# Latents' first norm written into the context's tiles, pinned squares and weight additions, and a last column block in two halves, in one transformer layer

## The chip, the cores and the metric

The kernel runs on one core of one Trainium2 chip. The metric is the device time of one execution in microseconds (us); the time before is 2582.37 us, the median of three runs from 2581.23 to 2585.36. The profile was taken from one further execution of 2582.33 us.

## The reference, cut to what matters

One layer of a hybrid backbone works on two streams of 256 tokens, the latents `x` and the context `ctx`, with 2048 features each:

```python
D_MODEL = 2048; SEQ = 256; CTX_LEN = 256; D_FF = 5632
def adaln(x, g, mod, i):
    return rms_norm(x, g) * (1 + mod[:, i + 1, None, :]) + mod[:, i, None, :]
def half_step_ffn(x, mod, i, g, w_up, w_down):
    h = adaln(x, g, mod, i)
    a, b = jnp.split(h @ w_up, 2, axis=-1)
    return x + 0.5 * mod[:, i + 2, None, :] * ((jax.nn.silu(a) * b) @ w_down)
...
xl = half_step_ffn(xl, mod_l, 0, g_norm[l, 0], w_ffn1_up[l], w_ffn1_down[l])   # FFN1, latents
xc = half_step_ffn(xc, mod_c, 0, g_norm[l, 0], w_ffn1_up[l], w_ffn1_down[l])   # FFN1, context
hl = adaln(xl, g_norm[l, 1], mod_l, 3)       # the second norm: input of the mixer
hc = adaln(xc, g_norm[l, 1], mod_c, 3)
...
xl = half_step_ffn(xl, mod_l, 6, g_norm[l, 2], w_ffn2_up[l], w_ffn2_down[l])   # FFN2, latents only
return rms_norm(xl, g_final)
```

`mod` is a vector of nine rows of 2048 per stream, each row a product of a condition vector with a weight matrix `w_mod`. Everything is float32.

## The kernel before, in words

**Precision and splits.** Each float32 operand of a matmul is split into a high and a low part, and each product is made of three matmuls (`mm3`: high by high, low by high, high by low). A weight tile of 128 x 2048 is split by `split` (L122) in two halves of 128 x 1024: ScalarE (ACT) copies the high part `hi` (L130), VectorE (DVE) subtracts it from the source into the low part `lo` (L131). TensorE (PE) takes the two parts as stationary operands: it can't run a low-part matmul before the `lo` of that half is done. Both `hi` and `lo` have four buffers.

**FFN1** (about 150 to 1060 us of the span) multiplies the up-projection as a seven-product scheme over 2x2 blocks. `quad(n)` runs over seven sums of activations (`a11`, `a12`, `n1`, `s4`, `s2`, `s3`, `a22`), each with two tiles of weights (`q` = 0, 1), which are also sums of weight blocks. Most of the weight sums are made by a DMA that adds into the tile in SBUF (`accum`, L742, on GpSimd's queue), some by DVE in halves of 1024 columns (`summed`, L912, its addition is recorded at L848). While this goes on, DVE also multiplies the modulation rows of `w_mod` (`sraw<-in_w_mt`, loads at L239 on SP's queue; two DVE operations of 128 x 1024 per load at L210, writing `junk`). Those run beside the matmuls, one item per step of the quad.

**FFN1's down-projection** ends in `last_pair` (about 1250 to 1370 us). `acc` holds four row tiles of 128 x 2048: tiles 0 and 1 are the context, 2 and 3 the latents. When a column block of a latents' tile is final, `kept` stores it to DRAM (`x1d<-acc`), since the latents' residual is read again later, and `stat` adds up its squares on ScalarE (`sumsq`, L163, recorded at L165, writing `junk`). `latents(c)` does both for the latents' tiles 2 and 3.

**The second norm** is `adaln(s)` (L1133), with s = 0 for the context and s = 1 for the latents: a reduction of the sums of squares on DVE (L1136, L1137), a power on GpSimd (POOL, L1138), then the tiles multiplied by the reciprocal root, the left half of each row tile on DVE (L1145), the right half on ACT (L1143), in place. `to_hT` transposes the result on PE in groups of eight 128 x 128 blocks (L378), and `affine_split` applies scale and shift, half of a group on ACT (L389) and half on DVE (L390), and splits the outcome (ACT L392 `hhi`, DVE L393 `hlo`). Matmuls of the mixer's input projection run between the groups. The context is normalised first; its tiles of `acc` are not read after its transposes.

**FFN2** (about 1930 to 2550 us) has its own `quad(n)`, nine of them; the sums of weights are made by `first`, `chained` and `accum` (DMA) and by `summed_half` (L2267, on DVE, recorded at L2212). The two pairs of weight tiles (`chain20/chain21` and `ra0/ra1`) change their places from one quad to the next, so that the profile writes `chain<-chain,ra` in one quad and `ra<-ra,chain` in the next. Between the quad's steps lie the matmuls of the down-projection of earlier blocks (`mm<-hi,hid2h`, with weights split from `raw`).

**The tail** is `last2`: for the last hidden blocks, the down-projection of two row tiles (t) in four column blocks of 512 (cb). For each block there are 12 matmuls, then DVE multiplies by the gate (`half_gated`, L1045, writing `sab`), adds into `acc2` (L2458), ACT adds up the squares (L165), and DVE multiplies the block before by the final gain (`gain`, L2426). When all four blocks of a row tile are done, `ended` reduces the four sums (L2431), adds the epsilon (L2433), has POOL take the power (L2434), scales the four blocks by the outcome (L2439, L2441 on DVE, L2443 on ACT) and stores them (L2444).

**What sets the order.** A scheduler orders the instructions of each engine by its own estimate of readiness, except those that `pin` or `pinned` (`keep_in_program_order`) hold in the order in which the code issues them. An addition or a square that isn't pinned may thus be put between the two halves of a split, or ahead of it.

Of the kernel before, what the change touches and what calls it, by code (L numbers as in the profile page):

```python
# [9 lines left out]
F32 = mybir.dt.float32  # L10
# [3 lines left out]
AF = mybir.ActivationFunctionType  # L14
# [46 lines left out]
def tile_layer(ctx: ExitStack, tc: tile.TileContext, I: dict, out: bass.AP):  # L61
# [13 lines left out]
    def bank():  # L75
        return ps["mm"].tile([P, 512], F32, tag="mm", name="mm")
# [85 lines left out]

    def sumsq(dst, x, n=512):  # L163
        junk = sm.tile([P, 512], BF16, tag="junk", name="junk", bufs=1)
        scalar[0].activation(junk[:, :n], x, AF.Square, accum_out=dst)  # L165

    def normalised(x, ss4, act=False):

# [170 lines left out]
    def pin(ins):  # L339
        tc.keep_in_program_order(ins)  # L340
# [30 lines left out]
    def to_hT(xs, n, s, hhi, hlo, c0, ks=range(KT)):  # L371

        for k0 in ks[::2]:
            tb = tbank()
            for kk in range(2):
                for t in range(2):
                    k = k0 + kk
                    tensor[0].transpose(tb[:, kk * 256 + t * P : kk * 256 + (t + 1) * P], xs[t][:, k * P : (k + 1) * P], ident)  # L378
            affine_split(tb.rearrange("p (k c) -> p k c", k=2), n, ((k0, s), (k0 + 1, s)), hhi[:, k0 : k0 + 2, c0 : c0 + 256], hlo[:, k0 : k0 + 2, c0 : c0 + 256])
            yield  # L380
# [334 lines left out]
    def pinned(ins):  # L715
        tc.keep_in_program_order(ins)
# [26 lines left out]
    with pool(name="f1u", bufs=1) as f1u:  # L743
# [110 lines left out]
        def quad(n, after=lambda step: None):  # L854
# [56 lines left out]

            def summed(q, h):  # L912
                w = slice(h * 1024, (h + 1) * 1024)
                add(chain_[q][:, w], chain_[q][:, w], ra[q][:, w])

            def second(q):
                if q not in own:
                    chained(1, 2)(q)
                if q - 1 in own:
                    summed(q - 1, 0)  # L920

            def third(q):
                if q in own:
# [209 lines left out]
    def adaln(s):  # L1133

        r = sm.tile([P, 16], F32, tag="rstd", name="rstd", bufs=4)[:, :2]
        nc.vector.tensor_reduce(r, ss1[s].rearrange("p (t c) -> p t c", t=2), axis=AX.X, op=ALU.add)  # L1136
        nc.vector.tensor_scalar(r, r, 1.0 / D, EPS, op0=ALU.mult, op1=ALU.add)  # L1137
        nc.gpsimd.tensor_tensor(r, r, mhalf[:, :2], op=ALU.pow)  # L1138
        for h in range(2):
            for t in range(2):  # L1140
                x = acc[:, 2 * s + t, h * 1024 : (h + 1) * 1024]
                if h:
                    nc.scalar.activation(x, x, AF.Copy, scale=r[:, t : t + 1])  # L1143
                else:
                    nc.vector.tensor_scalar(x, x, r[:, t : t + 1], None, op0=ALU.mult)  # L1145
        yield
        yield from to_hT([acc[:, 2 * s, :], acc[:, 2 * s + 1, :]], 1, s, *hT, 256 * s)

    hT = []

    def last_pair():
# [56 lines left out]
        def stat(t, cb):  # L1208
            s, tt = divmod(t, 2)
            if s not in ss1:  # L1210
                ss1[s] = sm.tile([P, 16], F32, tag="rstd", name="ss8", bufs=4)[:, :8]
            i8 = 4 * tt + cb
            sumsq(ss1[s][:, i8 : i8 + 1], col(t, cb))

        def kept(t, cb):
            if t > 1:
# [71 lines left out]
        def latents(c):  # L1288
            for t in (2, 3):
                kept(t, 2 * c + 1)  # L1290
                stat(t, 2 * c + 1)

        def last_small():
            small.update(zip(("s3", "a22"), pair_of(slot("nl"))))
# [768 lines left out]
    with f2x:  # L2063
# [146 lines left out]
        def quad(n):  # L2210
# [55 lines left out]

            def summed_half(q, h):  # L2267
                w = slice(h * 1024, (h + 1) * 1024)
                add(chain_[q][:, w], chain_[q][:, w], ra[q][:, w])

            def early(m, q):
                if (m, q) == (3, 0):
# [137 lines left out]
        def last2():  # L2410

            parts = []
            for cb in range(NCB):
                if cb >= 2:
                    parts.append(load_split(I["w_dn2"][LAST, cb]))
                    continue
                raw = raw_tile()
                nc.sync.dma_start(raw, I["w_dn2"][LAST, cb])
                hi = f3.tile([P, 2048], F32R, tag=f"f{2 * cb}", name=f"hi{cb}")
                lo = f3.tile([P, 2048], F32R, tag=f"f{2 * cb + 1}", name=f"lo{cb}")  # L2420
                nc.scalar.activation(hi, raw, AF.Copy)
                nc.vector.tensor_tensor(lo, raw, hi.bitcast(F32), op=ALU.subtract)
                parts.append(lambda w, hi=hi, lo=lo: (hi[:, w], lo[:, w]))
            def gain(t, cb):
                a = acc2[:, t, cb * CB : (cb + 1) * CB]
                pin(nc.vector.tensor_tensor(a, a, late["gf"][:, cb * CB : (cb + 1) * CB], op=ALU.mult))  # L2426

            def ended(t, ss):

                s1 = sm.tile([P, 1], F32, tag="s1", name="s1")  # L2430
                pin(nc.vector.tensor_reduce(s1, ss, axis=AX.X, op=ALU.add))  # L2431
# [17 lines left out]
            sss = [sm.tile([P, 4], F32, tag="ss4", name="ss4", bufs=4) for _ in range(2)]  # L2449
            first = ended(0, sss[0])  # L2450
            for t in range(2):
                for cb in range(NCB):
                    c = slice(cb * CB, (cb + 1) * CB)
                    b = block(bank(), LAST, parts[cb], t)
                    a = acc2[:, t, c]
                    y = sab_tile()
                    half_gated(y, b, late["g8"][:, c])
                    nc.vector.tensor_tensor(a, a, y, op=ALU.add)  # L2458
                    sumsq(sss[t][:, cb : cb + 1], a)
                    if cb or t:  # L2460
                        gain(*divmod(4 * t + cb - 1, 4))
                    if t:
                        steps(first)
            drain(ended(1, sss[1]))
# [101 lines left out]
```

## Time and profile before

| what | value |
|---|---|
| median of three runs | 2582.37 us (2581.23 to 2585.36) |
| the profiled execution | 2582.33 us |
| its span, first to last instruction | 2580.6 us, so 1.73 us lie outside |
| granted TensorE clock, mean | 0.999 |
| DVE busy | 86% of the span |
| ACT, POOL busy | 55%, 8% |
| mean DMA rate | 259 GB/s |

In a row of the timeline the first number is the start in us from the span's start, the second the busy time, then come engine, line, operation, output and inputs by the program's names (buffer numbers left out) and shapes; a bracket at the end is idle time of the engine just before, and what ended it. `x2` merges two instructions of one kind. PE's matmuls overlap: a 128 x 512 one is listed with 0.39 us and follows the one before by about 0.227 us.

### The profile page before, as it was taken

The numbers are of one execution on the slowest core, as the hardware profiler recorded it, in microseconds if no ns is written. First come the engines' busy times: TensorE is split into PE (matmuls) and PEld (weight loads), VectorE is DVE, ScalarE is ACT, GpSimd is POOL, SyncE is SP. The second block draws the span as 40 slices with busy tenths as digits, with TensorE's granted clock in tenths as the row PEclk, the third lists the DMA queues.
The fourth block names the chain that finished last, engine by engine and source line by source line (L and its number), as shares of the span: only waits on it lengthen the run. The fifth ranks groups of instructions, "written<-read, shape, count | busy, mean of one in ns | idle before, by whom it ended". The sixth has DMA issues, their size and how long they took to land.

```text
span 2580.6 us, 33786 instructions
## 1 busy us (share of the span) xinstructions
PE 2551.6 (99%) x12462; PEld 2117.9 (82%) x12462; DVE 2215.2 (86%) x2921; ACT 1407.3 (55%) x1805; POOL 214.9 (8%) x264
## 2 busy tenths in 40 slices
PE   8999999999999999999999999999999999999998
PEld 5788888888887888888889889888898888888886
DVE  7789888888889888888896889798889888888987
ACT  5454444444444455444464347566476666666763
POOL 0000000000000000011110000120000000000001
PEclk9999999999999999999999999999999999999999
DMA  9989999999999999999686887776768999999985
GB/s 397 353 213 263 260 274 253 250 275 272 261 269 255 264 258 247 244 211 235 162 200 247 314 293 258 244 261 224 265 251 236 274 276 283 286 276 272 272 252 167
DMA packets 150022, 668.97 MB, mean 259 GB/s; under 512 B 23000, under 2 KB 43992, under 8 KB 90336
## 3 DMA queue, kind: packets, MB, share of 16 engines
q1 hardware_dynamic: 121488, 484.34, 50.8%
q0 software_dynamic: 28368, 182.46, 35.9%
q8 instruction: 98, 1.61, 0.2%
q14 instruction: 68, 0.56, 0.1%
HBM read 648.86 MB, written 17.89 MB: 258 GB/s over the span
## 4 chain that ended last, share of the span: by engine, by line
PE 82%; DVE 7%; DMA 6%; issue 4%; ACT 1%; POOL 0%; ACTq 0%; POOLq 0%; DVEq 0%
PE mm L154 59%; PE Y L154 6%; PE X L154 5%; PE tr L154 3%; PE mm L89 3%; DVE lo L131 3%; PE tr L89 1%; DMA ra<-in_w_up2b 1%; DMA mraw<-in_w_m 1%; DMA chain<-in_w_dn 1%; DMA chain<-in_w_up1b 1%; DMA sr<-in_w_mt 1%; DVE junk L210 1%; ACT hi L130 1%; DMA raw<-in_w_dn 1%
## 5 line engine op out<-in xcount | busy, mean ns | idle before, releaser
L130 ACT ACTIVATE hi<-raw 128x1024 fp32r<-128x1024 f32 (+2 forms) x476 | 490.7, 1039 | 376.7 <-PE mm L154 278.8
L131 DVE TENSOR_TENSOR lo<-raw,hi 128x1024 fp32r<-128x1024 f32 (+2 forms) x464 | 553.0, 1205 | 94.9 <-ACT hi L130 77.2
L130 ACT ACTIVATE hi<-chain 128x1024 fp32r<-128x1024 f32 x352 | 369.1, 1059 | 332.9 <-PE mm L154 185.2
L131 DVE TENSOR_TENSOR lo<-chain,hi 128x1024 fp32r<-128x1024 f32 x352 | 425.0, 1220 | 101.0 <-ACT hi L130 93.3
L154 PE MATMUL mm<-hi,hhi 128*128 128x512 f32 (+3 forms) x1024 | 390.0, 381 | 0.0
L154 PE MATMUL mm<-lo,hhi 128*128 128x512 f32 (+3 forms) x1024 | 387.3, 378 | 1.2 <-DVE lo L131 0.8
L154 PE MATMUL mm<-hi,hlo 128*128 128x512 f32 (+3 forms) x1024 | 386.3, 377 | 0.0
L210 DVE SCALAR_TENSOR_TENSOR junk<-sraw,cBh 128x1024 fp8e5<-128x1024 f32 x192 | 234.6, 1222 | 24.4 <-DMA sraw<-in_w_mt 23.2
L154 PEld LDWEIGHTS mm<-lo,hhi 128*128 128x128 f32 x1024 | 192.4, 188 | 37.6 <-DVE lo L131 4.6
L154 PEld LDWEIGHTS mm<-hi,hhi 128*128 128x128 f32 x1024 | 192.5, 188 | 32.2 <-ACT hi L130 0.7
L154 PEld LDWEIGHTS mm<-hi,hlo 128*128 128x128 f32 x1024 | 192.6, 188 | 31.9
L131 DVE TENSOR_TENSOR lo<-ra,hi 128x1024 fp32r<-128x1024 f32 x104 | 126.3, 1222 | 27.5 <-ACT hi L130 23.6
L130 ACT ACTIVATE hi<-ra 128x1024 fp32r<-128x1024 f32 x104 | 110.0, 1061 | 65.7 <-PE mm L154 39.7
L154 PE MATMUL mm<-hi,sumshl 128*128 128x512 f32 x456 | 140.4, 389 | 0.0
L154 PE MATMUL mm<-lo,hid2h 128*128 128x512 f32 x352 | 137.3, 390 | 0.1
L154 PE MATMUL mm<-hi,hid2h 128*128 128x512 f32 x352 | 137.0, 389 | 0.0
L154 PE MATMUL mm<-hi,hid2l 128*128 128x512 f32 x352 | 137.0, 389 | 0.0
L154 PE MATMUL mm<-hi,sumshh 128*128 128x512 f32 x368 | 113.3, 389 | 0.0
L210 DVE SCALAR_TENSOR_TENSOR sr<-sr,cBl 128x1024 f32<-128x1024 f32 x84 | 102.1, 1224 | 12.7 <-DMA sr<-in_w_mt 11.8
L742 POOL DMA_DIRECT2D chain<-in_w_up1b x51 | 45.0, 883 | 738.2 <-DVE lo L131 591.3
L154 PE MATMUL mm<-hhi,hi 128*128 128x512 f32 (+1 forms) x288 | 101.4, 352 | 0.0
L154 PEld LDWEIGHTS mm<-hi,sumshl 128*128 128x128 f32 x456 | 85.6, 188 | 17.7
(526 smaller groups left out, 5431.3 us busy)
## 6 DMA issues: line engine op xcount, KB each, us to landing
raw<-in_w_dn SPq DMA_DIRECT2D x64, 1024.0 KB, 10.2
chain<-in_w_up1b POOLq DMA_DIRECT2D x51, 1024.0 KB, 10.9
sraw<-in_w_mt SPq DMA_DIRECT2D x96, 512.0 KB, 7.5
sr<-in_w_mt SPq DMA_DIRECT2D x81, 512.0 KB, 5.3
raw<-in_w_up1b SPq DMA_DIRECT2D x40, 1024.0 KB, 9.5
mraw<-in_w_m SPq DMA_DIRECT2D x32, 1024.0 KB, 7.5
chain<-in_w_dn POOLq DMA_DIRECT2D x28, 1024.0 KB, 9.7
chain<-in_w_up2b POOLq DMA_DIRECT2D x28, 1024.0 KB, 11.1
```

The costliest lines, as they stand in the source:

```text
L89: ins = getattr(self.engine, name)(*a, **k)
L130: scalar[0].activation(hi, src, AF.Copy)
L131: vector[0].tensor_tensor(lo, src, hi.bitcast(F32), op=ALU.subtract)
L154: tensor[0].matmul(out_ap, s, m, start=first and not n, stop=last and n == 2, skip_group_check=skip)
L210: ins = nc.vector.scalar_tensor_tensor(junk() if junk else raw, raw, 1.0, cB[s], op0=ALU.mult, op1=ALU.mult, accum_out=mT[:, i, s, kt, h : ...
L742: accum = lambda dst, src: nc.gpsimd.dma_start(dst, src, accum_op=ALU.add)
```

## The change

It has four parts.

1. `adaln` multiplies from tile `2s + t` into tile `t` of `acc`. For the latents (s = 1) the normalised values thus go into the context's tiles 0 and 1, and the transposes read from there; for the context nothing is different.
2. The squares that `latents` issues are pinned. All that the code issues ahead of them and that is pinned stays ahead.
3. In FFN1's `quad`, the addition `summed(q - 1, 0)` is pinned, behind the split that stands ahead of it in the code. In FFN2's `quad`, the first half of the second addition, `summed_half(1, 0)`, moves from step (3, 1) to step (2, 1) and is pinned there.
4. In the tail, the last column block of the second row tile (t = 1, cb = 3) is computed in two halves of 256 columns, each with its own bank, 12 matmuls, gate and addition; the first half's squares are taken by ACT, the second half's by DVE with a multiplication that accumulates. The sum of squares has five entries in place of four.

```diff
     def sumsq(dst, x, n=512):
...
-        scalar[0].activation(junk[:, :n], x, AF.Square, accum_out=dst)
+        return scalar[0].activation(junk[:, :n], x, AF.Square, accum_out=dst)
...
             def second(q):
                 if q not in own:
                     chained(1, 2)(q)
                 if q - 1 in own:
-                    summed(q - 1, 0)
+                    pinned(summed(q - 1, 0))
...
-                x = acc[:, 2 * s + t, h * 1024 : (h + 1) * 1024]
+                w = slice(h * 1024, (h + 1) * 1024)
+                x, y = acc[:, 2 * s + t, w], acc[:, t, w]
                 if h:
-                    nc.scalar.activation(x, x, AF.Copy, scale=r[:, t : t + 1])
+                    nc.scalar.activation(y, x, AF.Copy, scale=r[:, t : t + 1])
                 else:
-                    nc.vector.tensor_scalar(x, x, r[:, t : t + 1], None, op0=ALU.mult)
+                    nc.vector.tensor_scalar(y, x, r[:, t : t + 1], None, op0=ALU.mult)
         yield
-        yield from to_hT([acc[:, 2 * s, :], acc[:, 2 * s + 1, :]], 1, s, *hT, 256 * s)
+        yield from to_hT([acc[:, 0, :], acc[:, 1, :]], 1, s, *hT, 256 * s)
...
         def latents(c):
             for t in (2, 3):
                 kept(t, 2 * c + 1)
-                stat(t, 2 * c + 1)
+                pinned(stat(t, 2 * c + 1))
...
             def late_(m, q):
                 if (m, q) == (2, 1):
+                    pin(summed_half(1, 0))
                     summed_half(0, 0)
                 elif (m, q) == (3, 0):
                     accum(ra[0], part(n, 1, 0))
-                elif (m, q) == (3, 1):
-                    summed_half(1, 0)
...
+            def halves(t, cb, ss):
+
+                w = CB // 2
+                bs = [bank()[:, :w] for _ in range(2)]
+                y = sab_tile()
+                for h, b in enumerate(bs):
+                    o = cb * CB + h * w
+                    a, z = acc2[:, t, o : o + w], y[:, h * w : (h + 1) * w]
+                    tt = slice(t * P, (t + 1) * P)
+                    for j in range(FB):
+                        m = slice(j * CB + h * w, j * CB + (h + 1) * w)
+                        mm3(b, hids[LAST][0][:, j, tt], hids[LAST][1][:, j, tt], *parts[cb](m), j == 0, j == FB - 1)
+                    half_gated(z, b, late["g8"][:, o : o + w])
+                    nc.vector.tensor_tensor(a, a, z, op=ALU.add)
+                    if h:
+                        nc.vector.scalar_tensor_tensor(z, a, 1.0, a, op0=ALU.mult, op1=ALU.mult, accum_out=ss[:, cb + 1 : cb + 2])
+                    else:
+                        sumsq(ss[:, cb : cb + 1], a, w)
+                        gain(t, cb - 1)
...
             for t in range(2):
                 for cb in range(NCB):
+                    if (t, cb) == (1, NCB - 1):
+                        steps(first)
+                        halves(t, cb, sss[t])
+                        continue
```

Lines behind L1138 have numbers larger by one in the changed kernel. What moves on the engines is seen at three places.

ScalarE around the latents' squares of column block 1 (`junk,ss<-acc`), about 1330 us, where the context's norm is still being transposed (`h`, `hhi`) and weights are split (`hi`); before:

```order
L389 ACTIVATE h<-tr,SH,SC 128x256
L165 ACTIVATE junk,ss_10185<-acc 128x512 x2
L392 ACTIVATE hhi<-h 128x2x256
L389 ACTIVATE h<-tr,SH,SC 128x256
L1280 ACTIVATE hi<-raw 128x1024
L392 ACTIVATE hhi<-h 128x2x256
L1280 ACTIVATE hi<-raw 128x1024
```

The same engine and place in the changed kernel, from the same `h` on:

```order
L389 ACTIVATE h<-tr,SH,SC 128x256
L392 ACTIVATE hhi<-h 128x2x256
L389 ACTIVATE h<-tr,SH,SC 128x256
L1281 ACTIVATE hi<-raw 128x1024
L392 ACTIVATE hhi<-h 128x2x256
L165 ACTIVATE junk,ss_10185<-acc 128x512
L389 ACTIVATE h<-tr,SH,SC 128x256
L165 ACTIVATE junk,ss_10185<-acc 128x512
L1281 ACTIVATE hi<-raw 128x1024
```

The two squares stood together ahead of an `hhi`; now they come one by one, four to six instructions later. On PE the transposes of the third and fourth group after these draw together, in all as many as before.

VectorE in the third quad of FFN2, about 2094 us, where the second tile of the weight sum `n1` (`chain_15847`) is split and then takes the addition of `ra`; before:

```order
L2212 TENSOR_TENSOR chain_15846<-chain_15846,ra_15848 128x1024 x2
L131 TENSOR_TENSOR lo<-chain_15847,hi 128x1024
L2212 TENSOR_TENSOR chain_15847<-chain_15847,ra_15849 128x1024
L131 TENSOR_TENSOR lo<-chain_15847,hi 128x1024
L131 TENSOR_TENSOR lo<-raw,hi 128x1024 x2
```

And in the changed kernel:

```order
L2213 TENSOR_TENSOR chain_15846<-chain_15846,ra_15848 128x1024 x2
L131 TENSOR_TENSOR lo<-chain_15847,hi 128x1024 x2
L2213 TENSOR_TENSOR chain_15847<-chain_15847,ra_15849 128x1024
L131 TENSOR_TENSOR lo<-raw,hi 128x1024 x2
```

The addition moves behind the second `lo`; the `lo<-raw` behind both keeps its place in the count. Eight of the nine quads move like this. In the first quad, at 1961 us, one addition of `chain21` comes in ahead of the `lo<-raw` pair instead, and leaves its place two splits later.

VectorE in the FFN1 quad at 793 us (`chain_1337` and `chain_1338` are the quad's two weight tiles, `ca` a sum of activations, `junk,mT<-sraw,cBh` a product of modulation rows), one piece of the difference:

```order
 L848 TENSOR_TENSOR ca<-mm,ca 128x512
-L210 SCALAR_TENSOR_TENSOR junk_1342,mT<-sraw,cBh 128x1024
-L848 TENSOR_TENSOR ca<-mm,ca 128x512
-L131 TENSOR_TENSOR lo<-chain_1338,hi 128x1024 x2
-L210 SCALAR_TENSOR_TENSOR junk_1342,mT<-sraw,cBh 128x1024
+L131 TENSOR_TENSOR lo<-chain_1338,hi 128x1024
+L848 TENSOR_TENSOR ca<-mm,ca 128x512
+L131 TENSOR_TENSOR lo<-chain_1338,hi 128x1024
 L848 TENSOR_TENSOR chain_1337<-chain_1337,raw 128x1024
+L210 SCALAR_TENSOR_TENSOR junk_1342,mT<-sraw,cBh 128x1024 x2
 L131 TENSOR_TENSOR lo<-raw,hi 128x1024 x2
```

The two modulation products move behind the two halves of the split and the pinned addition. In four other quads of FFN1 (about 248, 325, 555 and 865 us) the first addition moves from between the two halves of `lo<-chain_1337` to a place behind two modulation products, which come one place ahead each; at 407 us one addition moves ahead of two splits; the other three quads with such an addition are as before. The order on GpSimd and SP is unchanged.

More of the change, by code (lines that the diff above doesn't have):

```diff
@@ L913, in summed @@
                 w = slice(h * 1024, (h + 1) * 1024)
-                add(chain_[q][:, w], chain_[q][:, w], ra[q][:, w])
+                return add(chain_[q][:, w], chain_[q][:, w], ra[q][:, w])
             def second(q):
@@ L1212, in stat @@
             i8 = 4 * tt + cb
-            sumsq(ss1[s][:, i8 : i8 + 1], col(t, cb))
+            return sumsq(ss1[s][:, i8 : i8 + 1], col(t, cb))
         def kept(t, cb):
@@ L2268, in summed_half @@
                 w = slice(h * 1024, (h + 1) * 1024)
-                add(chain_[q][:, w], chain_[q][:, w], ra[q][:, w])
+                return add(chain_[q][:, w], chain_[q][:, w], ra[q][:, w])
             def early(m, q):
@@ L2446, in ended @@
                         yield
-            sss = [sm.tile([P, 4], F32, tag="ss4", name="ss4", bufs=4) for _ in range(2)]
+            def halves(t, cb, ss):
[16 more added lines that the diff above has]
+                        gain(t, cb - 1)
+            sss = [sm.tile([P, 4], F32, tag="ss4", name="ss4", bufs=4), sm.tile([P, 16], F32, tag="rstd", name="ss5", bufs=4)[:, : NCB + 1]]
             first = ended(0, sss[0])
```

## The prediction

> **What bounds the kernel now.** The first part of the page, busy times, says which engine sets the time.
>
> ```profile
> PE 2551.6 (99%) x12462; PEld 2117.9 (82%) x12462; DVE 2215.2 (86%) x2921; ACT 1407.3 (55%) x1805; POOL 214.9 (8%) x264
> ```
>
> PE is busy in 2551.6 of 2580.6 us. The change takes no matmul away, so it can win back only part of the 29.0 us in which PE idles, and the stretch behind PE's last matmul. The view of waits, for PE, puts this down to its causes; its first row is the one that part 3 of the change bears on most:
>
> ```profile
> PE mm L154 <- DVE lo L131: 3.7, 7, 1.0
> ```
>
> Seven waits of `mm`, 3.7 us in all, end with a `lo` from DVE; a few of `Y` come to them. An addition between the halves of a split holds such a `lo` up by the time of one addition, but most of the time PE has enough in hand. So I read the timeline at every place where an instruction moves. To measure true losses there, PE's own pace is needed; these two matmuls of the timeline, in the tail, are twelve steps apart, so a step takes 2.72 / 12 = 0.227:
>
> ```profile
> 2567.67 0.39 PE L154 MATMUL mm<-lo,hid2h 128*128 128x512 f32 x1
> 2570.39 0.39 PE L154 MATMUL mm<-lo,hid2h 128*128 128x512 f32 x1
> ```
>
>  A change of 0.2%, 5.2 us, is about what a measurement of this kernel can tell from no change.
>
> **Part 1 and 2, the latents' norm.** ScalarE, DVE and PE (in this order) while the context's norm is transposed:
>
> ```profile
> 1332.92 0.63 ACT L165 ACTIVATE junk<-acc 128x512 bf16<-128x512 f32 x1 [1.71 <-DMA acc<-in_x]
> 1334.82 0.63 ACT L165 ACTIVATE junk<-acc 128x512 bf16<-128x512 f32 x1 [1.17 <-DMA acc<-in_x]
> 1336.09 0.69 DVE L393 TENSOR_TENSOR hlo<-h,hhi 128x512 fp32r<-128x512 f32 x1 [2.00 <-ACT hhi L392]
> 1337.16 1.22 DVE L131 TENSOR_TENSOR lo<-chain,hi 128x1024 fp32r<-128x1024 f32 x1
> 1338.43 0.50 PE L154 MATMUL mm<-lo,oddnh 128*128 128x512 f32 x1 [0.33 <-DVE lo L131]
> ```
>
> The two squares wait for residuals that a DMA adds into `acc`, hold `hhi` behind them, this holds DVE for 2.00 us, and DVE is late with a `lo` at 1338.38; PE waits. Its listed idle is 0.33; since a 128x512 matmul is listed 0.39 long but the next can follow after 0.227, the true loss is 0.33 + 0.16 = 0.49. With the squares behind `hhi` this goes: +0.49. The squares have time: their sum is wanted at 1356. That PE does two groups of transposes in one go behind them changes nothing that waits, since DVE and ACT take the groups one by one as before. The second place is the latents' norm itself (ScalarE, DVE, PE):
>
> ```profile
> 1359.48 2.19 ACT L1143 ACTIVATE acc<-acc,rstd 128x1024 f32<-128x1024 f32 x2 [3.28 <-DMA x1d<-acc]
> 1361.58 1.00 ACT L389 ACTIVATE h<-tr,SH,SC 128x256 f32<-128x256 f32 x2
> 1356.24 0.16 DVE L1136 TENSOR_REDUCE rstd<-ss 128x2 f32<-128x8 f32 x1 [0.85 <-ACT junk L165]
> 1357.51 1.42 DVE L1145 TENSOR_SCALAR acc<-acc,rstd 128x1024 f32<-128x1024 f32 x2 [0.90 <-POOL rstd L1138]
> 1362.16 1.00 DVE L390 TENSOR_SCALAR h<-tr,SC,SH 128x256 f32<-128x256 f32 x2 [3.23 <-ACT h L389]
> 1358.40 0.41 PE L378 MATMUL tr<-ident,acc 128*128 128x128 f32 x2 [1.12 <-DVE acc L1145]
> 1361.24 0.28 PE L154 MATMUL mm<-lo,hhi 128*128 128x256 f32 x1
> 1362.76 0.66 PE L378 MATMUL tr<-ident,acc 128*128 128x128 f32 x4 [1.23 <-DVE h L390]
> ```
>
> ACT's two halves write `acc` in place and so wait for the stores to `x1d` that read it, though the factor was there at 1357.51, when DVE began. `h` on ACT stands behind them and starts at 1361.58; DVE's `h`, with 3.23 idle, waits for it, and so PE's third group of transposes. With the output in the context's tiles nothing reads what is overwritten: the norms start with DVE's, and end some 2.2 later, well ahead of the first transposes' use. PE's last matmul before the wait starts at 1361.24 and the next could start about 0.11 later (half the step above), so 1.41 is lost here; I take 1.3 of it as won, with 0.1 left. Behind this place ACT and DVE alternate and set the pace of the remaining groups, as before: what is won here is won once. The wait at 1358.40 is a true 1.12 + 0.28 - 0.11 = 1.29; the chain squares, reduction, power, norm remains and gets earlier by what DVE wins at 1336.09. I take 0.85 of DVE's 2.00, the rest being used up by later waits; PE arrives 0.49 earlier, so 0.85 - 0.49 = 0.36 of this wait goes. Sum: 0.49 + 1.3 + 0.36 = 2.15, **+2.2 us**. Ends: 0.5, if only the first wait goes and the group cadence takes back the rest, and 0.49 + 1.29 + 1.41 = 3.2.
>
> **Part 3 in FFN2.** The third quad, DVE and then PE:
>
> ```profile
> 2094.15 1.23 DVE L2212 TENSOR_TENSOR chain<-chain,ra 128x1024 f32<-128x1024 f32 x1
> 2095.30 1.22 DVE L131 TENSOR_TENSOR lo<-chain,hi 128x1024 fp32r<-128x1024 f32 x1
> 2096.43 2.35 DVE L131 TENSOR_TENSOR lo<-raw,hi 128x1024 fp32r<-128x1024 f32 x2
> 2096.57 0.50 PE L154 MATMUL Y<-lo,n1f 128*128 128x512 f32 x1 [0.53 <-DVE lo L131]
> 2098.06 0.39 PE L154 MATMUL mm<-lo,hid2h 128*128 128x512 f32 x1
> ```
>
> The `lo` moves up by the addition's 1.15 (start to start), and PE's true wait of 0.53 + 0.16 = 0.69 goes. But the `lo<-raw` behind it still ends at 2096.43 + 1.22 = 2097.65, and PE needs it at 2098.06 now, at 2097.37 then: it binds next, and only 2098.06 - 2097.70 = 0.36 is left. Two more quads show such a wait:
>
> ```profile
> 2157.77 0.50 PE L154 MATMUL Y<-lo,n1f 128*128 128x512 f32 x1
> 2280.55 0.50 PE L154 MATMUL Y<-lo,n1f 128*128 128x512 f32 x1 [0.74 <-DVE lo L131]
> ```
>
> The last has the same order behind it and gets the same 0.36; the first has no listed idle, only the 0.50 that a matmul shows after a wait, so at most 0.16, and I take 0.16. The other five have slack: 0. The first quad goes the other way:
>
> ```profile
> 1961.41 1.23 DVE L2212 TENSOR_TENSOR chain<-chain,ra 128x1024 f32<-128x1024 f32 x1
> 1962.55 2.37 DVE L131 TENSOR_TENSOR lo<-raw,hi 128x1024 fp32r<-128x1024 f32 x2
> 1969.51 0.50 PE L154 MATMUL Y<-lo,s4f 128*128 128x512 f32 x1 [0.32 <-DVE lo L131]
> ```
>
> DVE has no gap there; one more addition ahead of 1962.55 moves all that follows by 1.14, PE already waits for `lo` at 1969.51, and the addition is taken out again only later. Of 1.14 I charge 0.85, since PE has other products to put ahead; ends 0 and 1.14. Sum: 0.36 + 0.36 + 0.16 - 0.85 = **0.0**; ends: 0.9 - 1.14 = -0.2 and, with the full waits, 0.69 + 0.9 + 0.16 = +1.8; downward I allow -1.1 if the gains vanish.
>
> **Part 3 in FFN1.** In four quads two additions and two products change places between splits that PE does not wait for now; the `lo` comes earlier, and the splits behind keep their place; what hides the moves is the matmuls of the halves already split, and without that cover each would cost up to the 1.14 of an addition. At 407 us an addition comes ahead of two splits, with the same cover. I take 0 for these five. The quad at 793 us is different (DVE, then PE):
>
> ```profile
> 799.47 1.23 DVE L848 TENSOR_TENSOR chain<-chain,raw 128x1024 f32<-128x1024 f32 x1
> 810.15 1.23 DVE L210 SCALAR_TENSOR_TENSOR junk<-sraw,cBh 128x1024 fp8e5<-128x1024 f32 x1 [2.50 <-DMA sraw<-in_w_mt]
> 813.84 0.50 PE L154 MATMUL mm<-lo,s2h 128*128 128x512 f32 x1
> 820.08 0.50 PE L154 MATMUL mm<-lo,s2h 128*128 128x512 f32 x1 [0.47 <-DVE lo L131]
> ```
>
> The product that frees `sraw` ended just before 799.47; it now stands behind the addition, 1.14 later. The load into that buffer lands so much later, DVE waits at 810.15 for it, and the `lo` that PE takes at 813.84 without slack is 1.14 late. Then the wait at 820.08, a true 0.47 + 0.16 = 0.63, is covered: 0.63 - 1.14 = **-0.5**; ends -1.1 and +0.4 (load not delayed, one small wait gone).
>
> **Part 4, the tail.** PE's last matmul above ends at 2570.78; 24 matmuls of half the width cost it hardly more, and the second half's gate comes over 1 us later. DVE runs without gaps (DVE's timeline, then groups by form):
>
> ```profile
> 2570.36 0.69 DVE L2426 TENSOR_TENSOR acc<-acc,gf 128x512 f32<-128x512 f32 x1
> 2570.96 0.69 DVE L1045 SCALAR_TENSOR_TENSOR sab<-mm,g 128x512 f32<-128x512 f32 x1
> 2573.22 0.16 DVE L2431 TENSOR_REDUCE s<-ss 128x1 f32<-128x4 f32 x1 [0.25 <-ACT junk L165]
> L1645 DVE SCALAR_TENSOR_TENSOR E<-mm,E 128x256 f32<-128x256 f32 x16 | 6.7, 416 | 0.7 <-POOL E L1630 0.6
> L390 DVE TENSOR_SCALAR h<-tr,SC,SH 128x256 f32<-128x256 f32 x16 | 8.6, 543 | 3.7 <-ACT h L389 3.2
> L89 DVE TENSOR_SCALAR xs<-xs,rstd 128x256 f32<-128x256 f32 x4 | 1.4, 347 | 0.4 <-POOL rstd L523 0.4
> ```
>
> From `sab` to the reduction it takes 2573.22 - 2570.96 = 2.26. After the change DVE has five instructions of 256 columns and one gain of 0.60 (2570.36 to 2570.96) in a row. The wait for ACT's square of 512 columns goes, but 256 columns cost more than half of 512: 0.416 to 0.69. With 0.44 for each: 5 x 0.44 + 0.60 = 2.80, **-0.55**. Ends by the rows of 0.347 and 0.543: 2.34 and 3.32, -0.1 and -1.05. I take the middle since the first row is nearest in kind.
>
> The Trainium skill ("VectorE: DVE Perf Modes", section "The TRN2 errata — SBUF-src ops pay a fixed extra latency per instruction") speaks against these halves: a fixed cost falls on each instruction, and tiles of 512 elements or more are advised. By its formula for float32 additions 256 columns take an estimated 424 ns, beside the 416 ns above, with which it agrees, and the tail would lose an estimated 0.46.
>
> **The sum.** 2.2 + 0.0 - 0.5 - 0.55 = +1.15, so 2582.33 - 1.2 = **2581.1 us**. The profiled execution and the median of the runs (2582.37) are 0.04 apart, so no correction.
>
> **The rivals.**
>
> (a) *All visible waits go, and nothing is charged*: 3.2 + 1.8 in FFN2 + 0.6 at 820.08 - 0.1 = 5.5, to 2576.8 us, just faster by over 0.2%. For it speaks that the waits are real; against it the `lo<-raw` at 2097.65 and the cadence of `h`, which bind next. 7%.
>
> (b) *Nothing of part 1 reaches the end* (only 0.5 of the 2.2 is kept, since DVE's later groups decide): 2582.33 - 0.5 + 1.05 = 2582.9 us. For it: behind 1362.76 ACT and DVE set the pace. Against: that pace starts earlier as well. 18%.
>
> (c) *Slower, by modulation loads in FFN1.* In the quad at 325 us a product of `sraw` moves up to where DVE now starts an addition (DVE, and the load's issue and landing):
>
> ```profile
> 324.66 1.22 DVE L848 TENSOR_TENSOR chain<-chain,raw 128x1024 f32<-128x1024 f32 x1
> L239 SPq DMA_DIRECT2D sraw<-in_w_mt x1: 351/351/351, 318.2 to 318.2; - x1
> DMA to landing us min/median/max: 8.8/8.8/8.8
> ```
>
> The load lands at 318.2 + 8.8 = 327.0; with the second `lo` ahead of it the product stands at about 325.8 and waits 1.2, which keeps DVE from the splits behind. Two products were to be done there anyway, so about 2.5 of delay is covered. If the load lands later than that in all four quads that move so, by as much as the 2.50 seen at 810.15 and 1.2 more, each costs some 2: 4 x 2 = 8, less the 1.2: 2589 us. It decides from a delay of 1.7 per quad on. Against it: the other three loads were issued long before. 4%.
>
> The forecast itself has 71%.
>
> **How the numbers follow.** Faster by over 0.2% (below 2577.2): most of (a), 0.06. Slower (above 2587.5): (c), 0.04. Within: 0.90. The range takes the four parts' ends, though not all at once: low 2577.5 (nearly (a)), high 2584.8, from 2582.33 - 0.5 + 1.1 (FFN2) + 1.1 (FFN1) + 0.8 (tail) = 2584.8.
>
> **What would show it.** In the profile after: no `x1d` behind ACT's norm, DVE's `h` at about 1360, and PE's transposes done some 2 us earlier; the wait at 2280.55 gone, but a short one for `lo<-raw` a little later; a longer wait for `lo` near 1965 to 1970; `sraw` landing near 811; 2.7 to 2.9 us between the last full gain's end and the reduction. The prediction is wrong if PE's idle falls by more than 4 us or grows, or if the time from PE's last matmul to the end shrinks.

## The result, and the profile after

The changed kernel takes 2577.74 us (median of 22 runs, 2575.09 to 2584.24) where before takes 2582.26 (22 runs). The ratio is 0.9984 with a 95% interval of 0.9978 to 0.9991: 4.1 us faster, between 2.3 and 5.7. The forecast was 1.2 us faster. Runs far above the others (two of before's 22, at 3642 and 4280 us, and further down the profiled run of `e2_ffn1`, at 4280 us) are left out of the ratios and readings. Time and sign lie where they were expected, but the time is only 0.2 above the low end of the stated range and the gain is more than three times the sum that was worked out, so the terms have to be gone through one by one.

The first part of the page after, and the view of stretches (before 150, FFN1, the rest; of before and, below it, of after). A row of that view gives the stretch, its length, the busy time of PE, PEld (PE's loads of stationary operands), DVE, ACT and POOL, the granted clock, the busy share of the DMA engines and their rate in GB/s:

```profile
PE 2546.7 (99%) x12474; PEld 2118.2 (82%) x12474; DVE 2216.2 (86%) x2925; ACT 1408.5 (55%) x1805; POOL 216.0 (8%) x264
```

```profile
0.00:150.00 150.00, 142.17 (x1054) 100.22 (x1055) 117.97 (x204) 69.68 (x128) 5.08 (x14) 1.00 0.94 357
150.00:1060.00 910.00, 906.19 (x3976) 743.99 (x3975) 795.80 (x986) 438.32 (x489) 75.93 (x87) 1.00 0.93 258
1060.00:2571.00 1511.00, 1503.29 (x7435) 1273.71 (x7433) 1298.01 (x1728) 897.00 (x1184) 133.34 (x163) 1.00 0.83 251
```

```profile
0.00:150.00 150.00, 139.45 (x1051) 98.59 (x1052) 117.12 (x203) 68.34 (x128) 4.23 (x14) 0.95 0.93 357
150.00:1057.00 907.00, 904.66 (x3980) 745.00 (x3979) 797.12 (x986) 440.46 (x489) 76.76 (x87) 1.00 0.94 259
1057.00:2565.00 1508.00, 1502.60 (x7447) 1274.60 (x7445) 1297.40 (x1727) 897.17 (x1183) 134.46 (x163) 1.00 0.83 252
```

PE's idle is 2575.8 - 2546.7 = 29.1 us, as before (29.0), though the span is 4.8 shorter. It fell in FFN1 (3.8 to 2.3) and behind it (7.7 to 5.4), and grew in the first 150 us, where the granted clock was 0.95 and nothing was changed. More is hidden in the busy time: a matmul is listed 0.39 long and could be followed after 0.227, so a wait of up to 0.16 counts as busy. Idle is therefore a poor measure here. A better one is the start of the same PE instruction in two profiles: how far PE is ahead at a place (its lead), and how this grows over a stretch. The table further down uses it.

The latents' norm after the change (ACT, DVE, PE), for the rows at 1357.51 to 1362.76 of before:

```profile
1332.32 0.63 ACT L392 ACTIVATE hhi<-h 128x512 fp32r<-128x512 f32 x1
1332.85 0.61 ACT L165 ACTIVATE junk<-acc 128x512 bf16<-128x512 f32 x1
1353.71 2.19 ACT L1144 ACTIVATE acc<-acc,rstd 128x1024 f32<-128x1024 f32 x2 [1.30 <-POOL rstd L1138]
1355.81 1.00 ACT L389 ACTIVATE h<-tr,SH,SC 128x256 f32<-128x256 f32 x2
```

```profile
1353.72 1.42 DVE L1146 TENSOR_SCALAR acc<-acc,rstd 128x1024 f32<-128x1024 f32 x2 [0.90 <-POOL rstd L1138]
```

```profile
1354.62 0.41 PE L378 MATMUL tr<-ident,acc 128*128 128x128 f32 x2 [0.80 <-DVE acc L1146]
1357.10 1.04 PE L378 MATMUL tr<-ident,acc 128*128 128x128 f32 x8
```

The square stands behind `hhi` and waits for nothing; ACT's norm starts with DVE's, at 1353.7, and is released by the power, no longer by a store; PE's third group of transposes starts without a wait, and the wait ahead of the first has shrunk from 1.12 to 0.80. All that was forecast. The rest of the gain is elsewhere.

### The profile page after: what moved, and what is told of

It is laid out like the page before. It is cut to its first block, busy times and chain, and to the rows that moved or that the text cites. A ratio compares the mean times of both kernels' runs of the same rounds, so it can differ in the third digit from the quotient of the medians.

```text
span 2575.8 us, 33817 instructions
## 1 busy us (share of the span) xinstructions
PE 2546.7 (99%) x12474; PEld 2118.2 (82%) x12474; DVE 2216.2 (86%) x2925; ACT 1408.5 (55%) x1805; POOL 216.0 (8%) x264
## 4 chain that ended last, share of the span: by engine, by line
PE 82%; DVE 8%; DMA 5%; issue 3%; ACT 2%; POOL 0%; ACTq 0%; POOLq 0%; DVEq 0%; SPq 0%
PE mm L154 59%; PE Y L154 7%; PE X L154 6%; PE tr L154 3%; PE mm L89 3%; DVE lo L131 3%; PE tr L89 1%; DMA chain<-in_w_up1b 1%; DVE junk L210 1%; DMA sr<-in_w_mt 1%; DMA chain<-in_w_dn 1%; ACT hi L130 1%; DMA raw<-in_w_dn 1%; DVE sr L210 1%; PE mm L1841 0%
## 5 line engine op out<-in xcount | busy, mean ns | idle before, releaser
L154 PE MATMUL mm<-lo,hid2h 128*128 128x512 f32 (+1 forms) x356 | 137.9, 387 | 0.4 <-DVE lo L131 0.4
L154 PE MATMUL mm<-hi,hid2h 128*128 128x512 f32 (+1 forms) x356 | 137.8, 387 | 0.0
L154 PE MATMUL mm<-hi,hid2l 128*128 128x512 f32 (+1 forms) x356 | 137.7, 387 | 0.0
## 6 DMA issues: line engine op xcount, KB each, us to landing
chain<-in_w_up2b POOLq DMA_DIRECT2D x28, 1024.0 KB, 10.6
```

The source lines that it names most:

```text
L154: tensor[0].matmul(out_ap, s, m, start=first and not n, stop=last and n == 2, skip_group_check=skip)
```

## The experiments

**Theory 1**: the four parts are worth what was worked out, and the surplus seen in FFN1 is chance in the landing of loads. **Theory 2**: the pinned additions of FFN1 are themselves worth some 3 us. Parts 1 and 2 together, the two places of part 3, and part 4 were run alone first.

Parts 1 and 2, `e1_norm_squares`, with the returns that `pinned` needs:

```diff
-                x = acc[:, 2 * s + t, h * 1024 : (h + 1) * 1024]
+                w = slice(h * 1024, (h + 1) * 1024)
+                x, y = acc[:, 2 * s + t, w], acc[:, t, w]
...
-        yield from to_hT([acc[:, 2 * s, :], acc[:, 2 * s + 1, :]], 1, s, *hT, 256 * s)
+        yield from to_hT([acc[:, 0, :], acc[:, 1, :]], 1, s, *hT, 256 * s)
...
-                stat(t, 2 * c + 1)
+                pinned(stat(t, 2 * c + 1))
```

> Parts 1 and 2 alone (latents' norm into the context's tiles, squares pinned). Theory 1 (parts as costed, the surplus in FFN1 is chance in the landing of loads): 2.2 us faster than before; PE's lead between the places of 1330 and 1370 us grows by 2.1 to 2.3; FFN1, whose code is as before, takes what it takes in any run of before, give or take 2 us. Theory 2 (FFN1's own moves are worth some 3 us): the same here, and the waits at about 791, 797, 820 and 920 to 997 us stay as in the profile of before.

Measured: 0.9998 (0.9986 to 1.0009). The profile shows 2.29 us of lead won between 1330 and 1379, and 1.7 lost in FFN1 and 1.9 between 1379 and 1930, where its code is as before. The part does what was said; a single median can't show 2 us against such swings.

Part 3 in FFN1, `e2_ffn1`, and again, `e2b_ffn1`:

```diff
                 if q - 1 in own:
-                    summed(q - 1, 0)
+                    pinned(summed(q - 1, 0))
```

> The pinned additions of FFN1 alone. Theory 1: between 0.5 slower and 0.5 faster; PE's waits in FFN1 come and go with the loads' landings, and from 60 to 1090 us the time differs from before's by chance only. Theory 2: about 3 us faster, with the waits at 791, 797, 820 and 920 to 997 us gone as in the profile after.

> The pinned additions of FFN1 alone, once more. The first four runs leave 7.1, 7.9, 9.4 and 9.6 us of lost PE starts between 150 and 1060 us where FFN1's code is as before, and 4.8 in the profile after. Theory 1 (chance): 7 to 10 us lost here too, and a time like before's. Theory 2 (the moves are worth some 3 us): 4 to 6 us lost, no waits at about 697 and 997 us, and 2 to 4 us faster than before.

Measured: 0.9990 (0.9981 to 0.9999) and 0.9990 (0.9981 to 0.9998), 2.6 us faster both times. The profile is that of `e2b_ffn1`. It is no faster in FFN1 than the first of before, and loses 8.4 us of PE starts there (the time from each 128x512 matmul's start to the next one's, beyond 0.227, summed over losses of 0.1 and more). The waits at 697 and 997 us, which theory 2 wanted gone, are there, 0.3 and 0.4 long. So the criterion by profile spoke for theory 1 and the time for theory 2.

Part 3 in FFN2, `e3_ffn2`:

```diff
                 if (m, q) == (2, 1):
+                    pin(summed_half(1, 0))
                     summed_half(0, 0)
...
-                elif (m, q) == (3, 1):
-                    summed_half(1, 0)
```

> FFN2's moved and pinned addition alone. Theory 1: 0 in sum; in the first quad PE loses 1.2 us between 1950 and 2010 (two waits for lo), in the quads at 2096, 2158 and 2281 it wins 0.7 to 0.9, 0.2 and 0.9, of which 0.4 is lost again behind the second. Rival (the later quads win without a loss): 1 us faster.

Measured: 1.0004 (0.9995 to 1.0012). The first quad costs 1.06 us of lead, by these two waits of PE:

```profile
1968.54 0.73 PE L154 MATMUL Y<-hi,s4f 128*128 128x512 f32 x2 [0.50 <-ACT cy L2226]
1974.47 0.50 PE L154 MATMUL Y<-lo,s4f 128*128 128x512 f32 x1 [0.65 <-DVE lo L131]
```

The waits at 2096, 2158 and 2281 are gone, but they are gone in `e1_norm_squares` and `e4_tail` as well, where these quads are as before. They can't be put down to the edit. What was said of the `lo<-raw` behind them, that it binds next, does happen with the edit, though behind the quad at 2158: in `after` (the row below) and in `e8b_best` PE loses 0.5 there, in `e3_ffn2` and `e8_best` nothing.

```profile
2155.10 0.50 PE L154 MATMUL mm<-lo,hid2h 128*128 128x512 f32 x1 [0.37 <-DVE lo L131]
```

Part 4, `e4_tail`, with the function `halves` as in the change:

```diff
+                    if (t, cb) == (1, NCB - 1):
+                        steps(first)
+                        halves(t, cb, sss[t])
+                        continue
```

> The tail's last block in halves alone. Theory 1: 0.6 us slower; from the first half's gate to the reduction 2.85 us on DVE where before takes 2.26, the rest as before. Rival (the shorter PE end counts): 0.3 faster or more. As time alone this lies below what five rounds tell; the profile decides.

Measured: 1.0000 (0.9991 to 1.0010). DVE in the tail:

```profile
2571.91 0.42 DVE L1045 SCALAR_TENSOR_TENSOR sab<-mm,g 128x256 f32<-128x256 f32 x1
2572.36 0.43 DVE L2462 TENSOR_TENSOR acc<-acc,sab 128x256 f32<-128x256 f32 x1
2572.70 0.68 DVE L2426 TENSOR_TENSOR acc<-acc,gf 128x512 f32<-128x512 f32 x1
2573.31 0.42 DVE L1045 SCALAR_TENSOR_TENSOR sab<-mm,g 128x256 f32<-128x256 f32 x1
2573.76 0.43 DVE L2462 TENSOR_TENSOR acc<-acc,sab 128x256 f32<-128x256 f32 x1
2574.22 0.42 DVE L2464 SCALAR_TENSOR_TENSOR sab<-acc 128x256 f32<-128x256 f32 x1
2574.75 0.16 DVE L2431 TENSOR_REDUCE s<-ss 128x1 f32<-128x5 f32 x1
```

From the first gate to the reduction 2574.75 - 2571.91 = 2.84, where before took 2.26: 0.58 lost, as worked out (0.55). In the changed kernel's profile it is 2.85.

How much of this reaches the end depends on how far DVE runs behind PE. In `e3_ffn2`, where the last block is whole, DVE waits for PE, and its gate starts 0.42 us behind the start of PE's last matmul (2572.75); below it, PE's last matmul of `e4_tail`:

```profile
2573.17 0.69 DVE L1045 SCALAR_TENSOR_TENSOR sab<-mm,g 128x512 f32<-128x512 f32 x1 [0.58 <-PE mm L154]
```

```profile
2572.19 0.28 PE L154 MATMUL mm<-lo,hid2h 128*128 128x256 f32 x1
```

In `e4_tail` the first half's gate, at 2571.91, starts ahead of PE's last matmul. A whole block, begun where the first half was (2569.43), would have its last matmul 11 steps of 0.227 later and its gate another 0.42 later, at an estimated 2572.35, so here the halves cost an estimated 0.1 and not 0.58. In the changed kernel DVE is so late that even the first half's gate starts 0.9 behind PE's last matmul, and the 0.58 counts in full. The two profiles of before differ in this as well: the last gate starts 0.57 and 1.27 behind PE's last matmul.

The two halves of the norm's part apart, `e5_norm` (only `adaln`) and `e6_squares` (only the pinned squares):

> The latents' norm into the context's tiles, squares not pinned. Theory (each of the two has its own waits): the wait at 1338 stays (0.5), the wait for h at 1363 falls from 1.4 to about 0.1, so 1.3 to 1.6 us of lead between 1330 and 1370. Rival (without the earlier squares the reduction comes later and the first wait takes the gain): under 0.7.

> The squares pinned, the norm in place as before. Theory: the wait at 1338 goes (0.5), but ACT's norm still waits for the stores to x1d and PE for h at 1363, as long as those stores land where they did: 0.5 to 0.9 us of lead between 1330 and 1370 at the most, or nothing if the wait at 1363 only grows by it.

Measured: 0.9995 (0.9986 to 1.0003) for each; in the profiles 1.18 and 0.62 of lead between 1330 and 1379, against 2.29 for both; `e5_norm` stays a little below the 1.3 to 1.6 that were expected. PE's waits there, of `e5_norm` and then of `e6_squares`:

```profile
1340.10 0.50 PE L154 MATMUL mm<-lo,oddnh 128*128 128x512 f32 x1 [0.53 <-DVE lo L131]
1360.07 0.41 PE L378 MATMUL tr<-ident,acc 128*128 128x128 f32 x2 [1.10 <-DVE acc L1146]
```

```profile
1356.25 0.41 PE L378 MATMUL tr<-ident,acc 128*128 128x128 f32 x2 [0.80 <-DVE acc L1145]
1360.91 0.66 PE L378 MATMUL tr<-ident,acc 128*128 128x128 f32 x4 [1.54 <-DVE h L390]
```

Without the pinned squares the first two waits stay and the third is gone; with the squares alone the first is gone, the second is 0.80, and the third has grown from 1.23 to 1.54, since ACT's norm still waits for the stores to `x1d` there. Each edit removes its own wait, and only together are both won whole (1.18 + 0.62 = 1.80, against 2.29).

Next, the change without the two parts that cost something, `e8_best`, run again as `e8b_best`: no `halves`, and in `late_`

```diff
                 if (m, q) == (2, 1):
-                    pin(summed_half(1, 0))
+                    if n > 1:
+                        pin(summed_half(1, 0))
                     summed_half(0, 0)
...
+                elif (m, q) == (3, 1) and not (n > 1):
+                    summed_half(1, 0)
```

> The change without the halves of the tail, and without the moved addition in FFN2's first quad. Theory: 0.6 (tail) and 1.2 (first quad) faster than the change, so 5 to 7 us faster than before; no waits for lo near 1960 to 1970 beside the one at 1969, 2.3 us from the last gate to the reduction; FFN1 loses 4 to 6 us as in the change. Rival (FFN1's gain was chance): 3 us faster than before, FFN1 losing 7 to 10.

> Once more the change without the tail's halves and without the moved addition in FFN2's first quad. Theory: 5 to 6 us faster than before, and 1 to 2 faster than the change. Rival (the first result was chance): 3 to 4 us faster than before.

Measured: 2576.48 and 2575.82 us, ratios 0.9979 (0.9971 to 0.9988) and 0.9978 (0.9969 to 0.9987), 5.4 and 5.7 us faster than before. DVE's tail is as before again, 2565.83 - 2563.57 = 2.26:

```profile
2563.57 0.68 DVE L1045 SCALAR_TENSOR_TENSOR sab<-mm,g 128x512 f32<-128x512 f32 x1
2565.83 0.16 DVE L2434 TENSOR_REDUCE s<-ss 128x1 f32<-128x4 f32 x1 [0.25 <-ACT junk L165]
```

This version beats before clearly, and its medians lie 1.3 and 1.9 us below the change's, near the 1.8 that the two parts cost at most; the intervals overlap.

FFN1's additions by quads, `e9_ffn1_late` (pinned for `n > 8` only: the quads at 793 and 865 us are changed) and `e10_ffn1_early` (for `n <= 8`: 248, 325, 407 and 555):

```diff
-                    pinned(summed(q - 1, 0))
+                    (pinned if n > 8 else lambda x: x)(summed(q - 1, 0))
```

> FFN1's pinned addition only in the last quads, of which those at 793 and 865 us differ from before. In all six profiles with FFN1 as before, the load of sraw issued near 800 us lands 10.4 to 10.6 us later, together with a chain load issued 0.8 earlier; in all three with the pinned addition it lands 7.0 to 7.1 later, the chain load being issued 3.2 earlier. Theory (these two quads hold what is systematic): 7.1 here too, PE 0.5 earlier between 785 and 830 and 1 us earlier between 900 and 960 than the mean with FFN1 as before; 1.5 to 2.6 us faster than before. Rival (chance, or the early quads): 10.4 and no difference.

> FFN1's pinned addition only in the earlier quads (248, 325, 407 and 555 us differ). Theory: the load near 800 us takes 10.4 to 10.6 as before, and the time is within 1 us of before. Rival (the early quads hold the gain): 2 to 3 us faster.

Measured: 0.9992 (0.9983 to 1.0001) and 1.0000 (0.9991 to 1.0009). The gain is in the late quads, if it is in either; the interval of `e9_ffn1_late` includes 1. The place near 800 us shows what the edit does to the loads. GpSimd's and SP's issues in before's timeline, and, below them, the time to landing of the first `sraw` load in the view of that tile:

```profile
798.82 0.87 POOL L742 DMA_DIRECT2D chain<-in_w_up1b  x1 [21.94 <-DVE lo L131]
799.59 6.14 SPq L239 DMA_DIRECT2D sraw<-in_w_mt  x2
```

```profile
DMA to landing us min/median/max: 10.5/10.5/10.5
```

The same of `e9_ffn1_late`, and its DVE and PE behind them:

```profile
799.30 0.88 POOL L742 DMA_DIRECT2D chain<-in_w_up1b  x1 [19.73 <-DVE lo L131]
802.47 0.33 SPq L239 DMA_DIRECT2D sraw<-in_w_mt  x1
```

```profile
DMA to landing us min/median/max: 7.3/7.3/7.3
```

```profile
794.20 1.23 DVE L848 TENSOR_TENSOR chain<-chain,raw 128x1024 f32<-128x1024 f32 x1
809.82 1.23 DVE L210 SCALAR_TENSOR_TENSOR junk<-sraw,cBh 128x1024 fp8e5<-128x1024 f32 x1 [0.42 <-DMA sraw<-in_w_mt]
817.74 1.23 DVE L210 SCALAR_TENSOR_TENSOR junk<-sraw,cBh 128x1024 fp8e5<-128x1024 f32 x1 [3.15 <-DMA sraw<-in_w_mt]
821.43 0.50 PE L154 MATMUL mm<-lo,s2h 128*128 128x512 f32 x1 [0.64 <-DVE lo L131]
```

The quad's first addition stands at 792.58 in before and at 794.20 here. From it, the chain load goes out after 6.2 us in before and 5.1 here, since the `lo` halves now precede the products; the `sraw` load after 7.0 and 8.3, since the products now follow the addition. So the two loads, 1 MB and 0.5 MB, start 0.8 apart in before and 3.2 apart here. In before both take 10.5; here they take 8.1 and 7.3, and `sraw` lands 1.9 earlier counted from the same addition, though it was issued 1.3 later. In all eight profiles without the late pinned additions it takes 10.4 to 10.6, in all five with them 7.0 to 7.3. The wait of DVE for it falls from 2.50 to 0.42. That the two loads share the DMA engines when they start together fits this, but was not tried apart from the order of the instructions. The Trainium skill ("DMA: Bandwidth & Descriptors", section "Queues, rings and completion order") says that each DMA engine takes turns between the queues that have work for it, a packet at a time; the landing times agree with that.

Little of these 1.9 us is kept, however. The next `sraw` load goes out 12.8 us after the addition in before and 13.0 here, and lands 23.7 and 23.4 after it, so DVE, early at the first product, waits the longer for the second: 3.15 in the rows above, where before has

```profile
816.39 1.23 DVE L210 SCALAR_TENSOR_TENSOR junk<-sraw,cBh 128x1024 fp8e5<-128x1024 f32 x1 [1.47 <-DMA sraw<-in_w_mt]
```

The two waits together are 3.9 to 4.1 in the eight profiles and 3.5 to 4.0 in the five. So the wait of PE at 820 stays.

The quad at 865 us gives more. There GpSimd's chain load goes out 1.4 to 1.8 us earlier in the five, counted against PE's own progress, and its next load lands 2.5 to 4.4 earlier. The `sraw` load of SP behind them is issued at the same place in all thirteen, at 901.38 in before, and takes 12.1 to 12.9 us to land in the eight and 10.6 to 10.9 in the five. The time to landing of that load, in before and in `e9_ffn1_late`, and the wait for it in before, which all eight have (0.45 to 1.11) and none of the five:

```profile
DMA to landing us min/median/max: 12.9/12.9/12.9
```

```profile
DMA to landing us min/median/max: 10.6/10.6/10.6
```

```profile
914.34 1.23 DVE L210 SCALAR_TENSOR_TENSOR junk<-sraw,cBh 128x1024 fp8e5<-128x1024 f32 x1 [0.45 <-DMA sraw<-in_w_mt]
```

That this load lands sooner because GpSimd's loads ahead of it were done sooner fits all thirteen, but was not tried apart either. `e9_ffn1_late` itself is 0.3 and 1.3 us ahead of the mean of the eight over the stretches from 785 to 830 and from 900 to 960, where 0.5 and 1 were expected, and 2.1 us faster than before by its time.

Last, the kernel before against itself:

> The kernel before against itself, a measure of chance. Theory: its ratio is 1 within 0.1%; its profile lies up to 2 us off the first one in several stretches, and the waits at 2096, 2158 and 2281 us, which five other profiles with these quads as before don't show, are absent here as well. Rival (the waits belong to the code): they are there.

Measured: 0.9994 (0.9986 to 1.0003), so 1.5 us can be chance. ACT at the FFN2 quad of 2094 us, in the first profile of before and in this one:

```profile
2091.80 2.01 ACT L130 ACTIVATE hi<-chain 128x1024 fp32r<-128x1024 f32 x2 [3.70 <-DMA chain<-in_w_up2b]
```

```profile
2089.26 2.14 ACT L130 ACTIVATE hi<-chain 128x1024 fp32r<-128x1024 f32 x2 [2.19 <-DMA chain<-in_w_up2b]
```

PE's matmuls there follow one another without a wait in this second profile:

```profile
2094.84 0.39 PE L154 MATMUL Y<-lo,n1f 128*128 128x512 f32 x1
2095.52 0.39 PE L154 MATMUL Y<-lo,n1f 128*128 128x512 f32 x1
```

The wait at 2096 on which FFN2's gains were built came from a load that landed late in one execution. The one at 2158 comes and goes in the eight other profiles with these quads as before: none in four, 0.1 to 0.2 in three, 0.8 in `e10_ffn1_early`.

The lead that PE wins (negative) or loses over a stretch, against the first profile of before, and what was changed in it. The norm's stretch ends at the first matmul that has the same place in all, at 1378.8 us in before, since the transposes ahead of it change their order:

| profile | FFN1, 150 to 1060 | norm, 1330 to 1379 | FFN2's first quad, 1930 to 2010 |
|---|---|---|---|
| e3_ffn2 | -0.51 | +0.55 | **+1.06** |
| e4_tail | +1.98 | -0.13 | +0.01 |
| e7_before | -0.92 | +0.57 | -0.01 |
| e1_norm_squares | +1.65 | **-2.29** | +0.04 |
| e5_norm | +0.61 | **-1.18** | +0.10 |
| e6_squares | -1.66 | **-0.62** | -0.01 |
| e10_ffn1_early | **-1.53** (early) | +0.40 | +0.03 |
| e9_ffn1_late | **-1.31** (late) | -0.07 | -0.01 |
| e2b_ffn1 | **+0.02** | +0.64 | +0.02 |
| after | **-3.66** | **-2.29** | **+1.40** |
| e8_best | **-3.26** | **-2.30** | 0.00 |
| e8b_best | **-5.45** | **-2.30** | +0.01 |

Bold is where the code differs from before in that stretch. The norm's gain and the first quad's loss repeat to a few tenths; where the norm's code is as before, its stretch still varies by 0.8 (-0.13 to 0.64). FFN1 swings by 3.6 us with the same code. With the first profile of before as 0, the eight without the late additions have a mean of -0.05, the five with them -2.73: 2.7 apart, with a standard error of 1.1. Single profiles don't tell the two groups apart: `e2b_ffn1`, with all the additions, is at 0.02, and `e10_ffn1_early`, with only the early ones, at -1.53.

## Why the prediction was right and wrong, point by point

- **Parts 1 and 2: right, in mechanism and size.** Worked out +2.2, measured 2.29 to 2.30 in four profiles. The three waits behave as said, and the two edits alone show that each has its own wait. Against the other profiles with the norm as before, which are 0.3 behind the first on average, the gain is nearer to 2.6.
- **Part 4: right in what DVE takes.** Worked out -0.55, measured -0.58. That all of it reaches the end was taken for granted; it holds in the changed kernel, but in `e4_tail` an estimated 0.1 of it does.
- **Part 3 in FFN2: wrong in size, 0.0 where -1.1 to -1.4 was measured.** The first quad costs 1.06 and 1.40, a little over the 0.85 charged. The step that failed is "The `lo` moves up by the addition's 1.15 (start to start), and PE's true wait of 0.53 + 0.16 = 0.69 goes": the wait at 2096 isn't there in seven of the eight other profiles with these quads as before, and is 0.1 long in the eighth; at 2281 there is 0.2 in the eighth and none in the seven. So the edit finds nothing to win there. From 2010 to 2550 PE wins 1.4 us on average in the four profiles with the edit and 2.3 in the eight without (all against the first profile of before), so no gain in the later quads shows.
- **Part 3 in FFN1: wrong in sign, -0.5 where +2.7 was measured by the profiles (standard error 1.1) and +2.6 by the time of its two runs.** The step that failed is "The load into that buffer lands so much later, DVE waits at 810.15 for it". The load is issued later, by 1.3, nearly the 1.14 that was said; it lands 1.9 earlier, now that it starts 3.2 behind the chain load and not 0.8. I had moved SP's issue and kept its landing time, and had not moved GpSimd's at all, though the same order of DVE sets both. The wait at 820, which was to be covered, stays in all five (0.5 to 1.1 lost, against 0.6 to 0.7 in the eight), since the next `sraw` load binds there. Behind the quad at 865, where the prediction took 0, PE wins 0.9 to 1.6 between 900 and 960 against the first profile of before in the five, and at most 0.9 (0.3 on average) in the eight. Of the 2.7 this is 1.1, and the stretch from 785 to 830 another 0.5, though there the two groups overlap; the rest, most of it behind 960, is not settled and may be chance.
- **The sum.** With the measured terms 2.3 + 2.7 - 1.2 - 0.6 = 3.2 us faster, within the measured 2.3 to 5.7. Without the two parts that cost, 5.0, where 5.4 and 5.7 were measured. That the time fell inside the stated range is in part luck: FFN1 gave more than the end of +0.4 that the range had for it, and FFN2's first quad took some of it back.
- **The rivals.** (a), all visible waits go, is near the measured time but not the reason: FFN2 gives none of its 1.8. (b) falls, since the norm's gain reaches the end of its stretch whole, and is not lost behind it: from 1379 to 1930 the five profiles with this norm lose 0.6 us on average, as do the eight without. (c), slower by loads in FFN1, falls: the early quads alone have a ratio of 1.0000, all of them 0.9990.
- **The signs to look for.** "The prediction is wrong if PE's idle ... grows" was no good test: it grew from 29.0 to 29.1, so by its letter the sign was there, while PE gained in the stretches that were changed. The time from PE's last matmul to the end did not shrink: it went from 9.9 to 10.9, and is 10.5 in the second profile of before. Of what was to be seen, ACT's norm without a wait for `x1d`, the earlier transposes, the longer wait for `lo` in FFN2's first quad (0.67 in place of 0.32) and 2.76 us from the last full gain's end to the reduction are there; `sraw` did not land near 811 but at 806.5.

## What to carry to other kernels

Where an edit moves an instruction that frees a buffer, move every load that this releases, on each queue, and ask which loads then start together: the landing time is not a constant of the load. Then follow the next load too, which may take back what the first one won. A wait of half a microsecond that ends on a transfer may exist in one execution only; a gain should be built on it only if a second profile of the same kernel shows it. And two edits that remove two waits in a row should be tried alone and together.

## What the runs showed that was not expected

Two loads of 1 MB and 0.5 MB issued 0.8 us apart both take 10.5 us to land; issued 3.2 us apart they take 8.1 and 7.3. FFN1, 910 us long with DMA engines busy 93% of it, takes from 1.7 us less to 2.0 us more in eight profiles that have these late quads in the same order, while the norm's stretch repeats to 0.01 us in the four profiles with both of its edits. And a load issued at the same place of PE's work, near 901 us, lands 1.2 to 2.3 us earlier when GpSimd's loads some 28 us ahead of it go out earlier.
